# Moving the S5 parameter set-up and two of its four weight sets from the first feed-forward network into the even mixer's output projection

## The chip, the core and the metric

The kernel runs on one core of a Trainium2 chip. Its engines have queues of their own, each worked off in order: TensorE (PE in the profile, its weight loads PEld), VectorE (DVE), ScalarE (ACT), GpSimd (POOL) and SyncE (SP), which only issues DMAs. The metric is the device time of one execution in microseconds (us), median over several runs. All arithmetic is in float32.

## The reference

The reference is a decoder trunk of two layers over a sequence of 512 positions and 1024 channels:

```python
for i in range(DEPTH):                      # DEPTH = 2
    hn = rms_norm(x, mix_norm[i])
    m = even_mixer(hn, ...) if i % 2 == 0 else odd_mixer(hn, ...)
    x = x + m
    x = x + conv_ffn(rms_norm(x, ffn_norm[i]), ...)
return rms_norm(x, final_norm)
```

The even mixer is retention (4 heads) beside a Mamba-2 state-space part (16 heads), joined to 2048 channels (`mix`) and mapped back by the output projection `mix @ w_out`. The odd mixer is a convolution module beside S5, a complex diagonal state-space model with 32 groups of 64 states. S5 needs parameters that depend on the inputs of the kernel alone and not on `x`:

```python
step = exp(log_step); mag = exp(a_re * step)
ab_re, ab_im = mag * cos(a_im * step), mag * sin(a_im * step)
f_re, f_im = ((ab - 1) / a)                 # real and imaginary part
bb = f * b                                  # complex, per state and channel
x[t] = ab * x[t-1] + bb @ u[t]; y = Re(c @ x) + d * u
```

The feed-forward network (FFN) is `(silu(gate) * up) @ w_down` with a convolution of width 3 behind the up-projection.

## The kernel before

The activations are held transposed: eight tiles `x[c]` of 128 channels by 512 positions. Each matrix product is done in three passes, on a split of both operands into a rounded part (`hi`) and the remainder (`lo`): `mm3` (L98) issues hi·hi, hi·lo and lo·hi. A weight block is loaded by SP (L89, tile `wraw`, four buffers), rounded by ACT (L90, `whi`, three buffers), and DVE subtracts (L91, `wlo`, three buffers). PE takes a block of 128 output channels in 12 matmuls where four tiles go in (the even output projection, `outp`, L566), and in 24 where eight go in (the FFN's up-projection).

**The even output projection.** The 16 `mix` tiles are projected four at a time, since groups of them are done at different times. `outs(k0, half)` (L583) takes the four tiles from `k0` on and four of the eight channel blocks; each `outp` ends in a DVE add into `x[c]` (L569, one operand in PSUM). With a third argument, `nst`, the block is the last one for that `x[c]`, and the next norm's work follows: `norm_chunk` (L155) makes `xh` (ACT, L161) and `xl` (DVE, L162) and adds the square (ACT L128 or L131, DVE L132). The last calls are `outs(0, 0)`, `outs(12, 0)`, `outs(4, 0, nst)`, `outs(4, 1)`, `outs(12, 1, nst)`: 20 blocks. The add of the last block of an earlier call, `outs(0, 1)`, is kept as `s5_mark`.

**The FFN's start.** In `ffn` (L172) step i of 22 takes two blocks of the up-projection. Behind the first block comes `norm_end` (L167): eight PE matmuls on the sums of squares (`pstat`, L138), DVE's reciprocal root (L140, L116 to L121), four PE transposes (`prow`, L147), and a DVE copy into `R` (L149). Each block's result is scaled by `R` (DVE L185, one operand in PSUM), convolved (ACT L187, two DVE instructions of L190, both tensor operands in SBUF), and after the pair, the gate (ACT L196, DVE L197) and a split (ACT L95, DVE L96) follow. Between the convolution and the gate, `next(aside)` (L194) runs one step of the generator `s5_prep`.

**The generator** (`s5_prep`, L613). Its first step is the set-up, which is queued behind `s5_mark` on DVE: small operations for `step`, `mag` and the angles (DVE, ACT's sine L670, L671), its tail (DVE L677 to L693), loads into `cdr`, `cdi` and `gt` (POOL DMAs, L696 to L700; DVE negates `cdi`, L698), and on POOL the powers of `ab` and the `bb` (`cmul`, L702 to L708, tile names `s5p`, `s5m`). Later steps call `weights(q)` (L759), a weight set: six POOL operations on 128x512 (L703 to L708 by way of L766) and six DVE products and sums (L768 to L773); `store(q)` (L776): four POOL DMAs to `w2d` (L780), eight PE transposes (L786), two ACT copies, two POOL DMAs to `w1d` (L788), eight small matmuls (pG) and a DVE add (L795); and `rot(h)` (L742). At the end `toep()` (L797) writes `tpd`; its zero stores (L802) need only the tile `zt`. The results go through DRAM and are read in the odd mixer.

**What sets the order.** Program order gives the priority. When the program is built, each engine's queue is ordered by it, and an instruction that isn't ready there gives way to a later one. Most tiles, those of the sets among them, come from one pool with 56 buffers (tag `slot`, L78). With `issue_after(ins)` instructions are queued behind `ins` on its engine.

Of the kernel before, what the change touches and what calls it, by code (L numbers as in the profile page):

```python
# [36 lines left out]
class Trunk:  # L37
# [249 lines left out]
        return st  # L287


    def even(self, st):  # L290
        nc = self.nc
        ins = self.ins
        C = self.c
# [272 lines left out]
        def outp(k0, c, last=None):  # L566
            p = self.pp("po")
            self.proj(p, ins["weo"][c, :, k0 * P:(k0 + 4) * P], mix[k0:k0 + 4])
            add = nc.vector.tensor_tensor(self.x[c], self.x[c], p, op=ALU.add)  # L569
            if last is not None:  # L570
                self.norm_chunk(last, c)
            return add
# [10 lines left out]
        def outs(k0, half, last=None):  # L583
            for c in range(4 * half, 4 * half + 4):
                self.add_mark = outp(k0, c, last)
# [15 lines left out]
        s5_mark = self.add_mark  # L601
        group_norm(1, grp[1], ys[1])
        head(3)
        outs(0, 0)
        outs(12, 0)
        outs(4, 0, nst)
        outs(4, 1)
        outs(12, 1, nst)
        self.add_mark = s5_mark
        return nst  # L610


    def s5_prep(self):  # L613
# [7 lines left out]
        def sm(shape=S16):  # L621
            n_[0] += 1
            return self.s5p.tile(shape, F32, name=f"s5_{n_[0]}")
# [6 lines left out]
        with self.tc.issue_after(self.dma_mark.ins), self.tc.issue_after(self.add_mark.ins):  # L630
# [7 lines left out]
            step, x, th, k, m1, m8, s, c, si, co = [sm() for _ in range(10)]  # L638
# [162 lines left out]
                if i:  # L801
                    dma(self.tpd[n:, :, i, :], zt[n:, :].rearrange("p (b x) -> p b x", b=8))  # L802

        for step in ((), (), (weights, 0), (), (store, 0, weights, 1), (), (store, 1, weights, 2), (), (store, 2, weights, 3),
                     (rot, 0), (store, 3), (rot, 1), ()):
            for f, q in zip(step[::2], step[1::2]):
                f(q)
            yield
# [381 lines left out]
def trunk(tc, ins, out):  # L1190
    from contextlib import ExitStack
    with ExitStack() as ctx:
        k = Trunk(ctx, tc, ins)
        st = k.load_x()
        st = k.even(st)
        st = k.ffn(0, st, "mix1", k.s5_prep())
        st = k.odd(st)
        k.ffn(1, st, "final", out=out)

# [15 lines left out]
```

## Time and profile before

| what | us |
|---|---|
| median of three timed runs (1360.03 to 1362.3) | 1360.99 |
| the profiled execution, its own time | 1361.88 |
| its span | 1360.1 |

By stage, in busy us:

| stretch (us from the span's start) | stage | PE | DVE | ACT | POOL |
|---|---|---|---|---|---|
| 0 to 413.5 | even mixer | 406.35 | 305.21 | 194.74 | 36.94 |
| 413.5 to 674.4 | first FFN, up-projection | 253.78 | 223.12 | 107.55 | 109.47 |
| 674.4 to 793.9 | first FFN, down-projection | 119.50 | 43.63 | 34.25 | 0.00 |
| 793.9 to 986.7 | odd mixer | 190.32 | 126.70 | 78.53 | 0.00 |
| 986.7 to 1360 | second FFN and final norm | 365.51 | 219.90 | 135.66 | 9.14 |

The granted clock of TensorE is 1.00 (full speed) in every stretch. A row of the timeline gives an instruction's start and duration in us, its engine, the line of the kernel, the operation, the tile written and those read, the shape, a count, and in brackets how long its engine had been idle and who ended that. Rows of one kind that follow each other are merged into one with their count.

### The profile page before, as it was taken

To read this page: it belongs to the slowest core of one execution; us is meant where nothing else is said; L and a number is where in the kernel's file an instruction comes from. 1 tells how busy PE (TensorE), PEld (TensorE's weight loads), DVE (VectorE), ACT (ScalarE), POOL (GpSimd) and SP (SyncE) were. 2 spreads that over 40 slices of the span, in tenths; PEclk is the share of its full clock that TensorE was granted. 3 is DMA by queue.
4 is the path that set the end of the run, shared out by engine and by line. 5 is a ranking of instruction groups with operands and counts; after the bars stand their busy time and mean duration, and the time that the engine had idled before them with its cause. 6 is when DMAs were issued, how large, how long until landed. Compare 5 with 4: busy or idle time off the path is not lost.

```text
span 1360.1 us, 17410 instructions
## 1 busy us (share of the span) xinstructions
PE 1335.5 (98%) x6660; PEld 1092.1 (80%) x6660; DVE 918.6 (68%) x1545; ACT 550.7 (40%) x775; POOL 155.6 (11%) x283
## 2 busy tenths in 40 slices
PE   8999999999999989999999999999999999999997
PEld 7778888888888777888888888657888888888887
DVE  5887877679568999977733345586877777774233
ACT  5454545444343444444422323144644444442221
POOL 0210010000306233870000000000000000000000
PEclk9999999999999999999999999999999999999999
DMA  6542223232234333553333335231432333233321
GB/s 224 156 111 84 70 81 123 77 104 83 77 119 142 109 109 109 170 160 97 97 90 96 102 95 197 86 143 55 124 109 93 95 102 98 93 90 96 101 71 62
DMA packets 50532, 146.16 MB, mean 107 GB/s; under 512 B 6544, under 2 KB 7872, under 8 KB 50448
## 3 DMA queue, kind: packets, MB, share of 16 engines
q1 hardware_dynamic: 44288, 127.49, 30.5%
q0 software_dynamic: 5872, 17.37, 4.5%
q8 instruction: 52, 0.85, 0.3%
q14 instruction: 32, 0.26, 0.1%
q10 hardware_dynamic: 288, 0.19, 0.0%
HBM read 135.03 MB, written 9.99 MB: 107 GB/s over the span
## 4 chain that ended last, share of the span: by engine, by line
PE 86%; DVE 10%; issue 2%; ACT 1%; DMA 1%; POOL 0%; DVEq 0%; SPq 0%; ACTq 0%; POOLq 0%
PE pup L102 9%; PE pup L100 9%; PE pup L101 9%; PE pdn L102 6%; PE pdn L100 6%; PE pdn L101 6%; DVE ffa L190 3%; PE po L100 3%; PE pcv L885 3%; PE po L102 3%; PE po L101 3%; DVE wlo L91 2%; PE pxbc L101 1%; PE pxbc L100 1%; PE pxbc L102 1%
## 5 line engine op out<-in xcount | busy, mean ns | idle before, releaser
L90 ACT CAST whi<-wraw 128x1024 fp32r<-128x1024 f32 (+3 forms) x246 | 231.0, 939 | 473.3 <-PE pdn L101 135.3
L91 DVE TENSOR_TENSOR wlo<-wraw,whi 128x1024 fp32r<-128x1024 f32 (+3 forms) x246 | 267.7, 1090 | 141.1 <-ACT whi L90 140.5
L102 PE MATMUL pup<-xh,wlo 128*128 128x512 f32 x704 | 274.6, 390 | 3.6 <-DVE wlo L91 3.6
L100 PE MATMUL pup<-xh,whi 128*128 128x512 f32 x704 | 275.0, 391 | 2.7 <-ACT whi L90 2.7
L101 PE MATMUL pup<-xl,whi 128*128 128x512 f32 x704 | 273.9, 389 | 0.0
L102 PEld LDWEIGHTS pup<-xh,wlo 128*128 128x128 f32 x704 | 132.1, 188 | 33.3 <-DVE wlo L91 5.7
L190 DVE SCALAR_TENSOR_TENSOR ffa<-ffh,c,ffa 128x511 f32<-128x511 f32 (+1 forms) x176 | 155.8, 886 | 2.9
L100 PEld LDWEIGHTS pup<-xh,whi 128*128 128x128 f32 x704 | 132.2, 188 | 30.3 <-ACT whi L90 3.5
L101 PEld LDWEIGHTS pup<-xl,whi 128*128 128x128 f32 x704 | 132.2, 188 | 27.2
L100 PE MATMUL pdn<-acth,whi 128*128 128x512 f32 (+1 forms) x374 | 140.9, 377 | 0.0
L101 PE MATMUL pdn<-actl,whi 128*128 128x512 f32 (+1 forms) x374 | 140.8, 377 | 0.0
L102 PE MATMUL pdn<-acth,wlo 128*128 128x512 f32 (+1 forms) x374 | 140.8, 377 | 0.0
L185 DVE TENSOR_TENSOR ffh<-pup,R 128x512 f32<-128x512 f32 x88 | 60.4, 687 | 57.2 <-PE pup L102 57.0
L232 POOL TENSOR_SCALAR x<-x,c 128x512 f32<-128x512 f32 (+1 forms) x9 | 9.1, 1016 | 738.7 <-ACT acc L128 639.3
L187 ACT ACTIVATE ffa<-ffh,c 128x512 f32<-128x512 f32 x88 | 71.8, 816 | 49.4 <-DVE ffh L185 46.2
L101 PEld LDWEIGHTS pdn<-actl,whi 128*128 128x128 f32 x374 | 70.4, 188 | 13.0
L102 PEld LDWEIGHTS pdn<-acth,wlo 128*128 128x128 f32 x374 | 70.4, 188 | 12.9
L100 PEld LDWEIGHTS pdn<-acth,whi 128*128 128x128 f32 x374 | 70.4, 188 | 12.8
L100 PE MATMUL po<-mh,whi 128*128 128x512 f32 x192 | 75.2, 393 | 0.7 <-ACT mh L95 0.7
L102 PE MATMUL po<-mh,wlo 128*128 128x512 f32 x192 | 75.6, 394 | 0.0
L101 PE MATMUL po<-ml,whi 128*128 128x512 f32 x192 | 75.5, 393 | 0.0
L95 ACT CAST acth<-ffg 128x512 fp32r<-128x512 f32 x44 | 27.3, 620 | 115.4 <-DVE ffg L197 110.8
(416 smaller groups left out, 2224.0 us busy)
## 6 DMA issues: line engine op xcount, KB each, us to landing
wraw<-in_wup_dram SPq DMA_DIRECT2D x88, 512.0 KB, 3.7
wraw<-in_wdn_dram SPq DMA_DIRECT2D x32, 512.0 KB, 3.5
wraw<-in_weo_dram SPq DMA_DIRECT2D x32, 256.0 KB, 3.1
wraw<-in_wxbc_dram SPq DMA_DIRECT2D x12, 512.0 KB, 3.7
wraw<-in_wdn_dram SPq DMA_DIRECT2D x16, 384.0 KB, 3.1
wraw<-in_wz_dram SPq DMA_DIRECT2D x8, 512.0 KB, 3.6
wraw<-in_wg_dram SPq DMA_DIRECT2D x8, 512.0 KB, 3.8
ar<-acd POOLq DMA_DIRECT2D x16, 256.0 KB, 3.9
```

Of the source, the lines that this page charges most:

```text
L90: nc.scalar.copy(hi[:, :n], raw[:, :n])
L91: (eng or nc.vector).tensor_tensor(lo[:, :n], raw[:, :n], hi[:, :n].bitcast(F32), op=ALU.subtract)
L95: self.nc.scalar.copy(hi, src)
L100: mm(out, lhsT=w[0], rhs=x[0], start=start, stop=False)
L101: mm(out, lhsT=w[0], rhs=x[1], start=False, stop=False)
L102: self.mark = mm(out, lhsT=w[1], rhs=x[0], start=False, stop=stop)
L185: nc.vector.tensor_tensor(h, p, st["R"], op=ALU.mult)
L187: nc.scalar.activation(a, h, AF.Identity, scale=dw[:, j, 2:3], bias=db[:, j:j + 1])
L190: nc.vector.scalar_tensor_tensor(a[:, s:], h[:, :T - s], dw[:, j, tap:tap + 1], a[:, s:], op0=ALU.mult, op1=ALU.add)
L232: self.nc.gpsimd.tensor_scalar(self.x[c][:, ts], self.x[c][:, ts], st["g"][:, c:c + 1], 1.0, op0=ALU.mult, op1=ALU.mult)
L885: self.mark = mm(p[64 * g:64 * g + 64, s:], lhsT=w, rhs=cin[i][g][:, :T - s], start=j == 0, stop=j == 15)
```

## The change

The generator is made before the even mixer and handed to it, and its first three steps are taken between the last blocks of the output projection: the set-up behind `outs(0, 0)`, weight set 0 behind `outs(12, 0)`, weight set 1 behind `outs(4, 0, nst)`. `self.add_mark` is set to the same `s5_mark` as before, earlier in the program. The list of steps is changed to go with it: the FFN's step 0 now stores set 0 (before: the set-up), step 1 stores set 1, step 3 makes set 2 (before: step 7), step 5 stores it, step 6 makes set 3 (before: step 9), step 8 stores it; the two rotations come at steps 9 and 11 (before: 10 and 12), and `toep()` at 13 (before: 14).

```diff
-    def even(self, st):
+    def even(self, st, prep):
...
         outs(0, 0)
+        self.add_mark = s5_mark
+        next(prep)
         outs(12, 0)
+        next(prep)
         outs(4, 0, nst)
+        next(prep)
         outs(4, 1)
         outs(12, 1, nst)
-        self.add_mark = s5_mark
         return nst
...
-        for step in ((), (), (weights, 0), (), (store, 0, weights, 1), (), (store, 1, weights, 2), (), (store, 2, weights, 3),
-                     (rot, 0), (store, 3), (rot, 1), ()):
+        for step in ((weights, 0), (weights, 1), (store, 0), (store, 1), (), (weights, 2), (), (store, 2), (weights, 3), (),
+                     (store, 3), (rot, 0), (), (rot, 1), ()):
...
-        st = k.even(st)
-        st = k.ffn(0, st, "mix1", k.s5_prep())
+        prep = k.s5_prep()
+        st = k.even(st, prep)
+        st = k.ffn(0, st, "mix1", prep)
```

## The prediction

> **What bounds the kernel now.** I read the page first, for the engines' shares; then the waits of TensorE (PE) and its order of time around the even mixer's output projection and the first feed-forward network (FFN); then VectorE (DVE) and GpSimd (POOL) in the same stretches, and last the busy time by stretch.
>
> ```profile
> PE 1335.5 (98%) x6660; PEld 1092.1 (80%) x6660; DVE 918.6 (68%) x1545; ACT 550.7 (40%) x775; POOL 155.6 (11%) x283
> ...
> 417.60:560.00 142.40, 135.28 (x631) 110.81 (x630) 131.17 (x165) 53.78 (x72) 69.74 (x103) 1.00 0.42 122
> ```
>
> PE is busy for 98% of the span of 1360.1 us, so the only time to be won without taking work away from PE is its idle time. The second row is the stretch in which the S5 parameters are now computed (columns: busy us of PE, PEld, DVE, ACT, POOL, granted clock, DMA share, GB/s). PE is idle for 142.40 - 135.28 = 7.1 us there; DVE is 92% busy. All of those 7.1 us stand in seven rows:
>
> ```profile
> 424.34 0.65 PE L147 MATMUL prow<-c,rs_y 128*128 128x128 f32 x4 [0.83 <-DVE rs_y L121]
> ...
> 444.51 0.50 PE L102 MATMUL pup<-xh,wlo 128*128 128x512 f32 x1 [0.67 <-DVE wlo L91]
> ...
> 479.07 0.50 PE L102 MATMUL pup<-xh,wlo 128*128 128x512 f32 x1 [1.38 <-DVE wlo L91]
> ...
> 504.99 0.50 PE L100 MATMUL pup<-xh,whi 128*128 128x512 f32 x1 [1.64 <-ACT whi L90]
> ...
> 506.50 0.50 PE L102 MATMUL pup<-xh,wlo 128*128 128x512 f32 x1 [0.78 <-DVE wlo L91]
> ...
> 531.82 0.50 PE L100 MATMUL pup<-xh,whi 128*128 128x512 f32 x1 [1.03 <-ACT whi L90]
> ...
> 533.34 0.50 PE L102 MATMUL pup<-xh,wlo 128*128 128x512 f32 x1 [0.78 <-DVE wlo L91]
> ```
>
> The first is the norm's end (0.83). The others come in four clusters, one behind each weight set: set 0 costs 0.67, set 1 1.38, set 2 1.64 + 0.78 = 2.42, set 3 1.03 + 0.78 = 1.81, together 6.28. In each, PE waits for a weight split that DVE (or ACT, behind DVE) made late. Why DVE was late stands in the rows of POOL and DVE around set 1:
>
> ```profile
> 468.58 0.63 POOL L780 DMA_DIRECT2D w2d<-w2i  x1
> 469.22 1.07 POOL L703 TENSOR_TENSOR w1r<-s5p,s5m 128x512 f32<-128x512 f32 x1
> ...
> 472.28 1.28 POOL L705 TENSOR_TENSOR w1r<-w1r,s5t 128x512 f32<-128x512 f32 x1
> ...
> 475.12 1.62 POOL L708 TENSOR_TENSOR w1i<-w1i,s5t 128x512 f32<-128x512 f32 x1
> ```
>
> ```profile
> 444.98 1.52 DVE L190 SCALAR_TENSOR_TENSOR ffa<-ffh,c,ffa 128x511 f32<-128x511 f32 x2
> ...
> 459.70 0.69 DVE L96 TENSOR_TENSOR actl<-ffg,acth 128x512 fp32r<-128x512 f32 x1 [0.69 <-ACT acth L95]
> ...
> 460.92 0.68 DVE L768 TENSOR_TENSOR w2r<-s5p,s5m 128x512 f32<-128x512 f32 x1
> ...
> 468.72 6.87 DVE L190 SCALAR_TENSOR_TENSOR ffa<-ffh,c,ffa 128x511 f32<-128x511 f32 x2
> 475.69 1.59 DVE L197 TENSOR_TENSOR ffg<-ffg,ffa 128x512 f32<-128x512 f32 x1
> 477.21 0.68 DVE L185 TENSOR_TENSOR ffh<-pup,R 128x512 f32<-128x512 f32 x1
> ```
>
> A weight set is six POOL operations on 128x512, from 469.22 to 475.12 + 1.62 = 476.74. While they run, two L190 and one L197, whose two tensor operands lie in SBUF, take 477.21 - 468.72 = 8.49 us; undisturbed two L190 take 1.52 (444.98), and a product of that size 0.68 (L768). A set therefore takes 8.49 - 2.20 = 6.3 us away from a DVE that has work. An operation of DVE with one operand in PSUM isn't held up:
>
> ```profile
> 565.20 1.06 POOL L703 TENSOR_TENSOR rotc<-rotc,s 128x256 f32<-128x256 f32 x1
> ```
> ```profile
> 565.70 0.68 DVE L185 TENSOR_TENSOR ffh<-pup,R 128x512 f32<-128x512 f32 x1
> ```
>
> **Where the moved work will stand.** The even output projection is 20 blocks of 12 matmuls, and DVE has room in some of them:
>
> ```profile
> 372.90:383.80 10.90, 10.90 (x50) 9.03 (x49) 5.16 (x8) 2.51 (x5) 0.00 (x0) 1.00 0.29 96
> 383.80:394.70 10.90, 10.90 (x49) 9.03 (x49) 9.62 (x15) 7.45 (x13) 0.00 (x0) 1.00 0.30 97
> 394.70:405.50 10.80, 10.80 (x49) 8.93 (x49) 5.25 (x9) 2.45 (x5) 0.00 (x0) 1.00 0.49 147
> 405.50:417.60 12.10, 12.10 (x55) 10.03 (x54) 11.63 (x16) 8.51 (x12) 0.00 (x0) 1.00 0.58 171
> ```
>
> In order these are outs(12,0), outs(4,0) with the norm's pieces, outs(4,1), and outs(12,1) with the norm's pieces. PE never waits; DVE's idle time is 10.90 - 5.16 = 5.74, 1.28, 5.55 and 0.47: half of a plain stretch is free, almost nothing of one with norm pieces.
>
> ```profile
> 372.95 0.69 DVE L569 TENSOR_TENSOR x<-x,po 128x512 f32<-128x512 f32 x1 [1.43 <-PE po L102]
> 373.56 0.69 DVE L91 TENSOR_TENSOR wlo<-wraw,whi 128x512 fp32r<-128x512 f32 x1
> 375.67 0.69 DVE L569 TENSOR_TENSOR x<-x,po 128x512 f32<-128x512 f32 x1 [1.43 <-PE po L102]
> ```
>
> A block is 375.67 - 372.95 = 2.72 us long. The split L91 behind a block's add belongs to the block three later (three wlo buffers); it ends at 374.25, and is first needed by the third matmul of a block that begins about 5.3 us after 372.95: at 378.6. DVE may thus be 4.4 us late before PE stops.
>
> Which of DVE's instructions comes when? The set-up's tail (L677 on) has its inputs from L655 at 341.12, and yet stands directly behind the last norm piece; and set 0's first product (L768, 460.92 above), which belongs to FFN step 3, stands just behind the split of step 2 (L96, 459.70):
>
> ```profile
> 341.12 0.17 DVE L655 SCALAR_TENSOR_TENSOR s<-s,s 128x16 f32<-128x16 f32 x1
> ...
> 368.56 0.68 DVE L96 TENSOR_TENSOR ml<-gs,mh 128x512 fp32r<-128x512 f32 x1
> ...
> 417.02 0.68 DVE L132 TENSOR_TENSOR acc<-acc,sq 128x512 f32<-128x512 f32 x1
> 417.62 0.18 DVE L677 TENSOR_TENSOR s5p<-s,s 128x16 f32<-128x16 f32 x1
> ...
> 419.09 0.18 DVE L692 TENSOR_TENSOR s<-s,s 128x16 f32<-128x16 f32 x1
> ...
> 422.64 0.28 DVE L693 TENSOR_SCALAR s5m<-s5m 128x256 f32<-128x256 f32 x1
> ...
> 428.34 1.18 DVE L698 TENSOR_SCALAR cdi<-cdi 128x512 f32<-128x512 f32 x1 [1.90 <-DMA cdi<-in_s5cdi_dram]
> ```
>
> ```profile
> 417.89 0.22 POOL L703 TENSOR_TENSOR s5p<-s5p 128x16 f32<-128x16 f32 x1 [57.45 <-DVE s5p L678]
> ...
> 430.42 4.24 POOL L802 DMA_DIRECT2D tpd<-s5z  x6
> 434.27 1.47 POOL L703 TENSOR_TENSOR w1r<-s5p,s5m 128x512 f32<-128x512 f32 x1
> ```
>
> I read it so: the tiles of tag "slot" are handed out in program order, and work that needs one follows. With the generator called earlier, L677 comes behind head(3)'s last split (L96, 368.56), near 369 to 371. POOL, which waited 57.45 us for it, needs 434.27 - 417.89 = 16.4 us from there to the first set, of which 4.24 and more are DMA issues that can go ahead; so set 0's POOL stream would begin near 381, and set 1's, which nothing separates from it, near 389, until 397: mostly over outs(4,0), the stretch with 1.28 us of room.
>
> **The sum.** Added to DVE between 371.5 and 417.6: the set-up's tail, 419.09 + 0.18 - 417.62 = 1.65 for L677 to L692, 0.28 for L693 and 1.18 for L698, 3.1 in all (L698's wait of 1.90 for cdi is left out, since the load can be issued earlier; with it 5.0, the upper bound); twelve products L768 to L773 at 0.61, the step from 372.95 to 373.56, 7.3; two POOL streams at 6.3, 12.6. Together 23.0. Against it stand the four idle times, 13.0, and the gap of 1.43 before 372.95: 14.5. At the end the norm's statistics allow a little:
>
> ```profile
> 418.99 0.95 PE L138 MATMUL pstat<-onec,acc 128*128 128x1 f32 x8
> ```
>
> PE comes to them at 418.99, the sum of squares is ready at 417.02 + 0.68 = 417.70: 1.3 more. So 23.0 - 14.5 - 1.3 = 7.2 us of DVE work find no room, and PE waits for it, in front of L91's splits late in outs(4,0) and in outs(4,1), and at pstat. The bounds of a stream's price: below, only the wait of the blocked splits, three per 8 us in plain blocks at 1.28 (L705's length) each, 3.8; above, all 7.5 from 469.22 to 476.74. I take 6.3, measured on this very stream.
>
> Won in the FFN: the norm's 0.83, since the set-up's operations no longer lie among the rsqrt's; I take 0.6, between 0 and 0.83. Of the 6.28, sets 0 and 1 are gone. Sets 2 and 3 now come at steps 3 and 6, their stores at 5 and 8. They may cost nothing, or what sets 2 and 3 cost now, 4.23. The nearest row is set 0, whose POOL stream also lay well ahead of its DVE products: 0.67 each, 1.3. Won: 6.28 - 1.3 = 5.0.
>
> At no cost I put: the two stores moved to steps 0 and 1 (the same transposes and matmuls of PE, copies of ACT and L795, and six POOL DMAs each, whose inputs were ready some 30 us before; if they weren't, PE, in order, would stand at the transposes); SP's queue, which is moved past nothing; and the seven zero stores of toep, POOL DMAs that go earlier and that nobody awaits. POOL's queue holds nothing else in the stretch (busy 0.00 in all four rows), so no DMA of another step is held behind the moved operations. No wait is added in the code; the new one is DVE's for its inputs from POOL, with the splits and adds queued behind it.
>
> Net: 7.2 - 0.6 - 5.0 = +1.6 us. The profiled execution took 1361.88 us (1.78 around its span), 0.9 above the median of the three timed runs, 1360.99. Its own time would become 1363.5; the median 1360.99 + 1.6 = 1362.6. About 0.2%, 2.7 us, is what a measurement of this kernel can tell from no change, so this is a trade that comes out even.
>
> [...]
>
> **The rivals.** *Slower: the FFN gives little back.* The two remaining sets each stand behind a store in POOL's queue, as sets 1 to 3 did, and DVE's six products (3.7 us) come against the stream (6.3), which is what made those sets cost 1.38 to 2.42 where set 0 cost 0.67. Price: the FFN still loses 4.23, and wins 2.05 instead of 5.0: 7.2 - 0.6 - 2.05 = +4.55, 1365.5. It decides from where the two cost over 2.4 us together (1.3, and the 1.1 from +1.6 to +2.7). For it: POOL's queue is in order, and a store's L780 waits for DVE. Against: a step without a set lies between. If the room of outs(4,1) also comes too late for the streams (5.55 less set 1's products, 3.7, so 1.9 more), 1367.4.
>
> *Faster: POOL can't hold DVE so long here.* Ahead of the stream at 469.22 POOL was issuing a DMA (L780, 468.58), in which L190 was already caught; in the projection no DMA need precede it, and if DVE gets in between POOL's instructions, a stream costs only 3.8: 23.0 - 12.6 + 7.6 - 15.8 = 2.2, and 2.2 - 0.6 - 5.0 = -3.4, 1357.6. Against it: L190 didn't get in between L703 and L705, where no DMA stood. [...]
>
> *Nothing moves:* the slots of the sets come free only at the end of the projection, POOL's streams stay at the FFN's start, and the time stays 1361. For it: this work waited for slots before (L677 above). Against: eight mix tiles are free after outs(0,0).
>
> **How the numbers follow.** Forecast 0.36, its own range 1360 to 1365 (the FFN's 0 to 4.23 around 1.3 cut at half); nothing moves 0.04; slower 0.36, since it needs only sets 2 and 3 to cost what they cost now; faster 0.24. So faster 0.24, same 0.40, slower 0.36. The range goes from a little below the faster case, 1356.5 (it, with sets 2 and 3 free, -1.3), to 1368, the slower case with the room missed.
>
> **What would show it.** Right: L677 near 369; POOL busy from 370 to 400; PE rows with 3 to 7 us of idle time in all, behind L91 between 385 and 410 and at pstat; L147's wait below 0.4; two clusters instead of four in the FFN, under 1 us each. Wrong: no idle PE in the projection (the streams' price falls), or clusters of 1.5 us and more behind sets 2 and 3, or POOL's streams still behind 417.

## The result and the profile after

The changed kernel takes 1368.72 us (median of four runs, 1368.68 to 1368.93) beside 1360.60 of the kernel before on the same chip: a ratio of 1.0060, 95% interval 1.0048 to 1.0073, so 8.1 us slower, outside the range given. (Lines from L609 on stand three further down in the changed kernel: L677 is L680, L698 is L701, L703 is L706, L768 is L771.)

First the engines' shares, then what TensorE waited for between 365 and 580 us (columns: us in total, times, longest), then the stretch of the FFN in which it was idle for 7.1 us before:

```profile
PE 1338.7 (98%) x6660; PEld 1095.0 (80%) x6660; DVE 913.2 (67%) x1545; ACT 551.3 (40%) x775; POOL 158.8 (12%) x283
```
```profile
PE po L102 <- DVE wlo L91: 11.3, 3, 5.7
```
```profile
417.60:560.00 142.40, 142.40 (x682) 119.27 (x682) 113.12 (x153) 62.59 (x83) 44.21 (x63) 1.00 0.46 134
```

The FFN's idle time is gone altogether (142.40 of 142.40), more than I gave it. Against that stand three stops, all in the projection, 11.3 us. In order of time, with what DVE and POOL did ahead of them:

```profile
384.67 0.80 PE L102 MATMUL po<-mh,wlo 128*128 128x512 f32 x1 [5.65 <-DVE wlo L91]
...
403.86 0.50 PE L102 MATMUL po<-mh,wlo 128*128 128x512 f32 x1 [2.53 <-DVE wlo L91]
...
414.31 0.66 PE L102 MATMUL po<-mh,wlo 128*128 128x512 f32 x1 [3.12 <-DVE wlo L91]
```
```profile
367.27 0.18 DVE L680 TENSOR_TENSOR s5p<-s,s 128x16 f32<-128x16 f32 x1
...
373.17 0.69 DVE L569 TENSOR_TENSOR x<-x,po 128x512 f32<-128x512 f32 x1 [1.31 <-PE po L102]
377.98 2.55 DVE L701 TENSOR_SCALAR cdi<-cdi 128x512 f32<-128x512 f32 x1 [4.12 <-DMA cdi<-in_s5cdi_dram]
380.45 4.17 DVE L91 TENSOR_TENSOR wlo<-wraw,whi 128x512 fp32r<-128x512 f32 x1
...
395.56 1.62 DVE L162 SCALAR_TENSOR_TENSOR xl<-x,c,xh 128x512 fp32r<-128x512 f32 x1 [0.19 <-ACT xh L161]
397.11 5.23 DVE L132 TENSOR_TENSOR acc<-acc,sq 128x512 f32<-128x512 f32 x1
...
408.76 0.69 DVE L771 TENSOR_TENSOR w2r<-s5p,s5m 128x512 f32<-128x512 f32 x1
...
413.57 0.69 DVE L91 TENSOR_TENSOR wlo<-wraw,whi 128x512 fp32r<-128x512 f32 x1
```
```profile
374.53 0.54 POOL L700 DMA_DIRECT2D cdi<-in_s5cdi_dram  x1
...
378.52 1.05 POOL L706 TENSOR_TENSOR w1r<-s5p,s5m 128x512 f32<-128x512 f32 x1
...
390.80 1.31 POOL L783 DMA_DIRECT2D w2d<-w2r  x2 [3.26 <-DVE w2r L773]
...
397.20 1.33 POOL L706 TENSOR_TENSOR w1r<-s5p,s5m 128x512 f32<-128x512 f32 x1
```

The first: DVE, which works its queue off in order, waits 4.12 us for `cdi`, whose load POOL issues only at 374.53, behind its powers of `ab`; then set 0's stream (from 378.52) holds L701 (2.55) and the split L91 (4.17). The second: set 1's stream (from 397.20) holds L132 (5.23). The third: set 1's six products and two adds stand in front of L91.

The stops aren't all. The next view is the busy time in stretches of 3.413 us; why this grid, is told below. The first pair is PE's busy us and matmuls, the clock is third from the end:

```profile
380.36:383.78 3.42, 0.00 (x0) 0.00 (x0) 3.42 (x2) 0.00 (x0) 3.41 (x4) 1.00 0.08 10
383.78:387.19 3.41, 2.52 (x6) 2.03 (x7) 3.41 (x4) 0.00 (x0) 3.40 (x5) 0.50 0.42 95
387.19:390.60 3.41, 3.41 (x9) 2.64 (x9) 3.41 (x6) 0.62 (x1) 0.35 (x1) 0.50 0.37 107
390.60:394.02 3.42, 3.42 (x16) 2.81 (x16) 3.42 (x6) 1.68 (x3) 2.12 (x4) 1.00 0.44 141
...
400.84:404.26 3.42, 0.89 (x5) 0.43 (x4) 3.42 (x4) 1.28 (x3) 3.26 (x3) 1.00 0.00 1
404.26:407.67 3.41, 3.41 (x10) 2.65 (x9) 3.22 (x5) 1.40 (x3) 0.69 (x1) 0.50 0.24 77
407.67:411.08 3.41, 3.41 (x16) 2.57 (x14) 3.41 (x6) 1.87 (x4) 0.00 (x0) 1.00 0.23 77
411.08:414.50 3.42, 0.30 (x2) 0.19 (x2) 3.42 (x7) 0.09 (x1) 1.88 (x3) 1.00 0.40 77
414.50:417.91 3.41, 3.41 (x9) 2.66 (x9) 1.55 (x3) 0.00 (x0) 0.70 (x2) 0.50 0.68 156
```

Behind each stop PE is granted half the clock for one or two such stretches, and a full one then holds 9 or 10 matmuls instead of 16. PE is "busy" there, so no view of waits shows it. Lost: half of 2.52 + 3 x 3.41, 6.4 us.

Together 11.3 + 6.4 - 7.1 = +10.6. The profiled execution of before had come to the projection some 2.3 us later than that of the changed kernel, with nothing changed ahead of it (the first matmul of `pxbc` by L102 starts at 21.72 there and at 19.42 in the changed kernel; L147 starts at 424.34, and in run e3 below, which changes nothing ahead of it either, at 421.99), which leaves 8.3.

```profile
421.99 0.65 PE L147 MATMUL prow<-c,rs_y 128*128 128x128 f32 x4 [0.83 <-DVE rs_y L121]
```

Those 2.3 us come from the clock at the start of the run. PE begins at 5.06 us in the execution of before and at 4.92 in that of the changed kernel, but its matmuls come twice as close (0.13 us from start to start instead of 0.23) only from 12.86 us on in the one and from 8.31 in the other; half of the difference is 2.3 us. At these times the clock record of the two traces has its first entry, so the 1.00 that a view gives for the time ahead of it says nothing; the counts of matmuls in the same stretch do (before, then after):

```profile
9.00:11.00 2.00, 2.00 (x9) 2.00 (x10) 2.00 (x4) 2.00 (x5) 0.00 (x0) 1.00 1.05 393
```
```profile
9.00:11.00 2.00, 2.00 (x19) 2.00 (x18) 2.00 (x4) 2.00 (x4) 0.00 (x0) 1.00 1.05 390
```

The spans differ by 6.8, 1.5 us less than the 8.3. Half of that lies in how a row counts idle time, from the modelled end of the matmul before it: from start to start the stops cost 11.8 us here and 8.3 before. The rest stays open.

### The profile page after: what moved, and what is told of

The parts are those of the page before. It is cut to its first block, busy times and chain, and to the rows that moved or that the text cites. A ratio compares the mean times of both kernels' runs of the same rounds, so it can differ in the third digit from the quotient of the medians.

```text
span 1366.9 us, 17413 instructions
## 1 busy us (share of the span) xinstructions
PE 1338.7 (98%) x6660; PEld 1095.0 (80%) x6660; DVE 913.2 (67%) x1545; ACT 551.3 (40%) x775; POOL 158.8 (12%) x283
## 4 chain that ended last, share of the span: by engine, by line
PE 92%; DVE 5%; ACT 1%; issue 1%; DMA 0%; POOL 0%; DVEq 0%; ACTq 0%; POOLq 0%
PE pup L100 12%; PE pup L102 12%; PE pup L101 12%; PE pdn L100 6%; PE pdn L102 6%; PE pdn L101 6%; PE pcv L888 3%; PE po L100 2%; PE po L102 2%; PE po L101 2%; PE pxbc L101 1%; PE pxbc L100 1%; PE pxbc L102 1%; PE pyd L454 1%; PE pqk L100 1%; PE pqk L102 1%
## 5 line engine op out<-in xcount | busy, mean ns | idle before, releaser
L91 DVE TENSOR_TENSOR wlo<-wraw,whi 128x1024 fp32r<-128x1024 f32 (+3 forms) x246 | 271.9, 1107 | 141.3 <-ACT whi L90 140.9
L102 PE MATMUL pup<-xh,wlo 128*128 128x512 f32 x704 | 274.0, 389 | 0.0
L102 PEld LDWEIGHTS pup<-xh,wlo 128*128 128x128 f32 x704 | 132.1, 188 | 27.5
L102 PE MATMUL pdn<-acth,wlo 128*128 128x512 f32 (+1 forms) x374 | 140.8, 377 | 0.0
L190 DVE SCALAR_TENSOR_TENSOR ffa<-ffh,c,ffa 128x511 f32<-128x511 f32 (+1 forms) x176 | 135.9, 773 | 3.0
L102 PE MATMUL po<-mh,wlo 128*128 128x512 f32 x192 | 78.3, 408 | 11.3 <-DVE wlo L91 11.3
L102 PEld LDWEIGHTS pdn<-acth,wlo 128*128 128x128 f32 x374 | 70.4, 188 | 12.9
```

Source lines behind the costliest of these rows:

```text
L91: (eng or nc.vector).tensor_tensor(lo[:, :n], raw[:, :n], hi[:, :n].bitcast(F32), op=ALU.subtract)
L102: self.mark = mm(out, lhsT=w[1], rhs=x[0], start=False, stop=stop)
L190: nc.vector.scalar_tensor_tensor(a[:, s:], h[:, :T - s], dw[:, j, tap:tap + 1], a[:, s:], op0=ALU.mult, op1=ALU.add)
```

## Experiments

Line numbers are those of each run's own kernel (L703 of before is L704 in e2 and L706 in e12). *Lookahead* is how late DVE may be before PE stops, 4.4 us by the prediction.

Theory A: DVE's lateness makes the stops, in pieces (the wait for `cdi` with set 0's stream, set 1's stream, its products), and TensorE's clock is halved behind each long one. Rival B: the amount of DVE work and the streams count, wherever the pieces are cut. Rival C: the lower clock costs nothing.

**The disputed cost by itself.** 18 idle DVE additions (nobody reads them) in the kernel before, in one piece, then in two.

```diff
         outs(0, 0)
+        hold(18)                # e6: hold(9)
         outs(12, 0)
         outs(4, 0, nst)
+                                # e6: hold(9)
```

> The kernel before with nothing moved and 18 extra DVE additions of 128x512 in one piece behind outs(0,0), on tiles that nobody reads: 18 x 0.61 = 11.0 us in which the splits wait. Less the gap of 1.43 us and the lookahead of 4.4 us that makes one TensorE stop of about 5.2 us. Theory A (the clock is granted by fixed windows of 3.41 us, and is halved behind a window in which TensorE worked less than about 0.45 of the time, for one to three windows): a stop of 5 us always empties one window, so that the time grows by 5.2 + 1.7 to 3.4 for each half-clock window or two, 7 to 9 us in all: 1367 to 1369. Rival C (a granted clock of 0.50 is a matter of record): 5.2 us, 1365.4.

Measured: 1366.86, ratio 1.0047 (1.0034 to 1.0059), +6.5 us. The timeline of DVE and the stretches of the grid (PE first, clock third from the end):

```profile
369.73 10.92 DVE L609 TENSOR_TENSOR dyb<-dya 128x512 f32<-128x512 f32 x18
```
```profile
377.47:380.89 3.42, 0.00 (x0) 0.00 (x0) 3.42 (x7) 0.00 (x0) 0.00 (x0) 1.00 0.00 0
380.89:384.30 3.41, 2.92 (x7) 2.17 (x8) 3.35 (x6) 0.00 (x0) 0.00 (x0) 0.50 0.06 19
384.30:387.71 3.41, 3.41 (x17) 2.83 (x16) 1.29 (x2) 0.62 (x1) 0.00 (x0) 1.00 0.63 210
```

The stop was 4.8 us, near the 5.2 of gap and lookahead, and half clock followed for one window, 1.5 us. Theory A's 3.41 us is the grid of the changed kernel's trace, and its 0.45 lies between a window busy for 0.42 in e4 that half clock followed and one busy for 0.46 in e3 that full clock followed. By the total alone the rival's 5.2 isn't excluded; the count of matmuls, and e4 below, exclude it.

> The same 18 additions as two pieces of 9, behind outs(0,0) and behind outs(4,0): 5.5 us each. Theory A: each is under the gap of 1.43 us and the lookahead of 4.4 us together, so TensorE stops for under 0.5 us in all, no window is emptied, and the time stays within 1 us of the kernel before, 1360 to 1361: the room of the projection is real, if it is used in pieces. Rival B (the amount of work counts, 11 us against a room that the norm's pieces use up): half of the cost of the one piece, 1363 and more.

Measured: 1362.52, ratio 1.0014 (1.0006 to 1.0023), +2.1: between the two. PE stopped 0.15 us behind the first piece, and 1.11 + 0.41 behind the second, which follows the norm's pieces, where DVE arrives late. The same work costs a third in two pieces. The interval, 1361.2 to 1363.5, still holds the rival's 1363; that the cut matters at all is shown by 2.1 beside 6.5.

**One cause of the first stop taken away.** The loads of `cdr`, `cdi`, `gt` go out behind the set-up's first loads.

```diff
                 nc.gpsimd.dma_start(t_, ins[n])
...
+            dma(cdr, ins["s5cdr"])
+            dma(cdi, ins["s5cdi"])
...
+            dma(gt, ins["s5dd"])
...
-            dma(cdr, ins["s5cdr"])
-            dma(cdi, ins["s5cdi"])
...
-            dma(gt, ins["s5dd"])
```

> Only the issue of the three small loads (cdr, cdi, gt) moves: behind the set-up's first loads instead of behind POOL's power chain. Theory A (in-order wait plus clock): DVE's 4.12 us wait for cdi goes, the first stop of TensorE in the projection falls from 5.65 us to under 2, and the half clock of some 6 us behind it (2.9 us lost) goes with it: about 7 us less than the changed kernel, 1361 to 1363; the stops of 2.53 and 3.12 us stay, each with half clock behind. Rival B (only the amount of DVE work and the POOL streams count): the wait is filled, but the stream of set 0 then meets the same splits, so at most the 4 us come back and more likely 1 to 2: 1365 to 1368. Rival C (the granted clock is a matter of record and costs nothing): 4 us, 1364.5, with the matmuls' spacing as in the changed kernel.

Measured: 1366.76, ratio 1.0049 (1.0037 to 1.0062): only 2.0 less than the changed kernel (1.5, each taken beside its own runs of the kernel before), the rival's number. The wait is gone, and with DVE earlier at them, the products of set 0 met the stream in front of the adds:

```profile
380.79 2.99 DVE L771 TENSOR_TENSOR w2r<-s5p,s5m 128x512 f32<-128x512 f32 x1
383.70 4.04 DVE L772 TENSOR_TENSOR s5u<-s5p,s5m 128x512 f32<-128x512 f32 x1
387.67 1.82 DVE L774 TENSOR_TENSOR w2i<-s5p,s5m 128x512 f32<-128x512 f32 x1
```

One piece of 9 us; stops of 3.1 and 3.8 follow, and one of 4.9 behind splits that set 1's stream held (6.28 us for two): 11.8 us in sum, no less than the 11.3 with the wait. That the wait for `cdi` by itself cost the first stop, as I held, falls.

**Less of the change.** e2 moves the set-up alone, and calls the sets at the FFN's steps of the kernel before; e4 leaves set 1 to the FFN's step 0.

```diff
         outs(12, 0)
-        next(prep)              # e2 only
         outs(4, 0, nst)
-        next(prep)
```

> Only the set-up is moved into the projection; the sets stay at the FFN's steps of the kernel before. Theory A: the 4.12 us wait for cdi stands in front of the splits, but no stream follows it, so that of the 4.4 us that DVE may be late little is exceeded: one stop of 0 to 2 us, no half clock behind it; the norm's 0.83 us in the FFN goes, the four clusters (6.3 us) stay: 1360 to 1362, no difference to the kernel before. Rival B (the set-up by itself is what makes the first stop): a stop of 4 us and more and half clock: 1366 and more.

Measured: 1356.38, ratio 0.9971 (0.9961 to 0.9982), 3.8 faster and below theory A's 1360 to 1362, which had left all four of the FFN's clusters standing. The wait for `cdi` (3.86) makes a stop of 1.43 us, at full clock (1.00 from 378 to 392); in the FFN one cluster was left of four (1.0 + 0.8). Set 0, called at FFN step 3, ran in the projection all the same, since POOL's queue held nothing else:

```profile
384.71 1.46 POOL L704 TENSOR_TENSOR w1r<-s5p,s5m 128x512 f32<-128x512 f32 x1
```
```profile
384.73 5.26 DVE L91 TENSOR_TENSOR wlo<-wraw,whi 128x512 fp32r<-128x512 f32 x1
```

It held a split for 5.26 us, and PE stopped for 0.15 us: one hold alone is all but covered.

> Set-up and set 0 stay in the projection, set 1 goes back to the FFN's step 0. Theory A: the first stop (5.65 us and half clock behind it) stays, the second and third (2.53 and 3.12 us, and 3.4 us of half clock) go: 9 us less than the changed kernel, 1359 to 1361, a little faster than before or equal, if the FFN's three sets cost nothing. Rival C (half clock costs nothing): 5.7 us less, 1363.

Measured: 1363.44, ratio 1.0022 (1.0013 to 1.0031): 5.3 less than the changed kernel (4.8, each taken beside its own runs of the kernel before), the rival's number, but not for its reason. Two stops stayed, 9.0 us in sum, the longer one 5.6, since set 1's stream, called later, began at 398.23 all the same (397.20 in the changed kernel), over L132; only the products' stop went. This run shows the cost of the clock. Its eleven executions differ in their mean granted clock, and in time with it:

| mean granted clock | executions | us |
|---|---|---|
| 0.997 | 2 | 1360.96, 1361.08 |
| 0.995, 0.996 | 6 | 1362.94 to 1363.70 |
| 0.994 | 3 | 1364.56 to 1364.75 |

0.003 of 1363 us are 4.1 us; the time grows by 3.6. With the counts of matmuls above, the granted clock is no mere record. The mean alone would not show it: in the kernel before, executions at 0.997 and at 0.998 take the same time (1359 to 1361 us), and five of eight at 0.999 take longer, 1361.7 to 1362.6; the mean leaves out the time ahead of the clock record's first entry.

**The FFN's side.** e3 moves nothing, and spaces the steps.

```diff
-        for step in ((), (), (weights, 0), (), (store, 0, weights, 1), (), (store, 1, weights, 2), ...
+        for step in ((weights, 0), (), (store, 0), (weights, 1), (), (store, 1), (weights, 2), ...
```

> Nothing is moved into the projection; in the FFN the four sets and the four stores stand in steps of their own (sets at steps 1, 4, 7, 10, stores at 3, 6, 9, 12). Theory A (what the FFN won came from the spacing, not from having two sets fewer): all four clusters go, PE idle time in the FFN falls from 7.1 us to about 1: 1354 to 1356. Rival B (it came from having two sets fewer there): the sets that DVE's products follow at once still cost 0.7 to 2.4 each, 1358 to 1361.

Measured: 1358.15, ratio 0.9985 (0.9976 to 0.9994), the rival's end: stops of 0.83, 0.59, 0.46 and 2.87 were left. The last shows that length alone doesn't decide on the clock:

```profile
476.07:479.48 3.41, 2.39 (x11) 1.66 (x9) 3.41 (x7) 1.76 (x2) 1.32 (x2) 1.00 0.24 43
479.48:482.89 3.41, 1.56 (x7) 1.29 (x8) 3.41 (x5) 0.92 (x2) 1.25 (x2) 1.00 0.65 95
482.89:486.31 3.42, 3.42 (x17) 2.81 (x16) 2.59 (x5) 1.44 (x3) 0.00 (x0) 1.00 0.82 303
```

It falls over two windows, of which neither is emptied (busy for 0.70 and 0.46), and the clock stays at 1.00; behind the 2.53 us in the changed kernel, all in one window (busy for 0.26), it was 0.50.

**No POOL stream at all.** The sets' six multiplications and sums go to DVE: e7 in the changed kernel; e8 with set-up alone moved and loaded early, sets at FFN steps 0, 3, 6, 9; e11 the same sets with nothing moved.

```diff
...
-            cmul(v(w1r), v(w1i), pw(qr), pw(qi), mt(bbr), mt(bbi), v(t1))
+            cmul(v(w1r), v(w1i), pw(qr), pw(qi), mt(bbr), mt(bbi), v(t1), nc.vector.tensor_tensor)
```

> The changed kernel with the six multiplications and sums of every weight set on DVE instead of POOL; places and steps as in the changed kernel. DVE then has 12 x 0.61 = 7.3 us a set and no stream holds it, instead of 3.7 of its own and 5.2 to 6.3 held. Theory A (the streams' holds, in one piece each, make the stops; the half clock follows from their length): stops of 1 to 3 us behind the wait for cdi and behind the second set, 2 to 6 us in all, at most one or two half-clock windows: 1354 to 1361, 1357 likeliest. Rival B (the place is full, whoever does the work): the three stops stay as they are, 1366 to 1369.

Measured: 1366.02, ratio 1.0041 (1.0027 to 1.0054), the rival's side: five stops, 7.9 us, and a mean granted clock of 0.994, as in the changed kernel's trace. Eleven of set 1's twelve instructions came as one piece, from 403.69 to the add at 410.32, and the next rows of DVE show three adds and three splits caught up one behind the other:

```profile
409.72 0.68 DVE L775 TENSOR_TENSOR s5u<-s5p,s5m 128x512 f32<-128x512 f32 x1
410.32 0.68 DVE L569 TENSOR_TENSOR x<-x,po 128x512 f32<-128x512 f32 x1
410.92 0.68 DVE L776 TENSOR_TENSOR w2i<-w2i,s5u 128x512 f32<-128x512 f32 x1
411.52 1.28 DVE L569 TENSOR_TENSOR x<-x,po 128x512 f32<-128x512 f32 x2
412.71 1.89 DVE L91 TENSOR_TENSOR wlo<-wraw,whi 128x512 fp32r<-128x512 f32 x3
```

So the streams are not the root either: a piece of 7 us of DVE's own work at this place stops PE as well.

> Set-up alone in the projection, with its three small loads issued early; all four sets in the FFN, on DVE, at steps 0, 3, 6 and 9, and each store in a step of its own. Theory A: no stop in the projection, and 0 to 2 us of idle time of TensorE in the FFN in place of 7.1: 1352 to 1355. Rival B (12 instructions of DVE in one piece are 7.3 us, more than the splits may be late): a stop of 1 to 2.5 us for each set, 1356 to 1361.

Measured: 1350.95, ratio 0.9928 (0.9916 to 0.9941), 9.5 us faster than before: the version that beats both. PE waits for nothing between 365 and 580 us. The same twelve instructions a set that stop PE in the projection cost nothing in the up-projection; a likely reason is that a `wlo` buffer there holds a block of 24 matmuls (twice 2.72 us), here one of 12.

> Nothing moved into the projection; the four sets in the FFN on DVE, at the same distance from each other as in the run with the early set-up (1350.95). It tells what the move of the set-up is worth by itself. Theory A: the norm's 0.83 us stays and the sets cost nothing: 1351.5 to 1353. Rival: the set-up in the FFN makes DVE and POOL late for set 0, a stop of 1 to 3 us: 1353 to 1356.

Measured: 1355.80, ratio 0.9961 (0.9947 to 0.9975), the rival's number: a stop of 2.1 us behind set 0 and the norm's 0.8 (mean granted clock 0.997 in this trace, 0.998 in e8's). Moving the set-up, with its loads issued early, is worth the 4.9 us to e8.

**More lookahead.** Four buffers instead of three for `whi` and `wlo`, in the changed kernel (e9) and in the kernel before (e10).

```diff
-        hi = self.wp.tile([P, 1024], F32R, name="whi", tag="whi", bufs=3)
-        lo = self.wp.tile([P, 1024], F32R, name="wlo", tag="wlo", bufs=3)
+        hi = self.wp.tile([P, 1024], F32R, name="whi", tag="whi", bufs=4)
+        lo = self.wp.tile([P, 1024], F32R, name="wlo", tag="wlo", bufs=4)
```

> The changed kernel with four buffers instead of three for the split weights (whi and wlo), so that a split may run one block further ahead: 2.72 us more in the projection, 7.1 instead of 4.4. Theory A (a stop is what a piece of DVE work exceeds the lookahead by, and half clock follows where a window is emptied): the stops of 5.65, 2.53 and 3.12 us fall by up to 2.7 each, to about 2.9, 0 and 0.4, and two or three of the five half-clock windows go: 7 to 12 us less than the changed kernel, 1357 to 1362. Rival B (DVE has too much work in the projection; buffers don't help): the lateness adds up, stops of 9 to 11 us stay, 1365 to 1369.

Measured: 1368.14, ratio 1.0053 (1.0040 to 1.0065), no gain, and the rival's number. The first stop fell from 5.65 to 2.93, one block as expected; at the second place another limit took over:

```profile
PE po L102 <- DVE wlo L91: 4.5, 2, 2.9
PE po L100 <- DVE x L569: 4.0, 2, 3.3
```

PE then waits for the adds of `po` that stand behind the held L132 (5.21 us; there are four such accumulators), and the mean granted clock stays at 0.994.

> The kernel before with the same four buffers, as the control of the run beside it: the four clusters behind the sets in the FFN (6.3 us) are a lateness of DVE as well; a block there is 5.45 us, and one more buffer covers more than the longest of them (2.42). Theory A: the 6.3 us go, the norm's 0.83 stays: 1353 to 1355. Rival B: no difference, 1360.

Measured: 1354.66, ratio 0.9958 (0.9946 to 0.9971), as theory A had it: one stop of 1.7 and the norm's 0.9 were left. In the FFN lookahead alone wins back 4.5 of the 7.1 us of idle time that the change won there.

**A set in pieces.** As e8, but set 0's products go behind the second block of outs(12, 0), the rest of it behind the first of outs(4, 1).

```diff
+                if c == at:
+                    next(prep)
...
-        outs(12, 0)
+        outs(12, 0, at=1)
         outs(4, 0, nst)
-        outs(4, 1)
+        outs(4, 1, at=4)
```

> Set-up (loads early) and set 0 in the projection, set 0 on DVE in two pieces of six instructions, 3.7 us each: the products behind the second block of outs(12, 0), the other six behind the first block of outs(4, 1), where DVE is idle half of the time; sets 1 to 3 in the FFN on DVE. Theory A (a piece under the gap of 1.43 and the lookahead of 4.4 costs nothing): no stop in the projection, the time of the run with set-up alone moved, 1350 to 1352. Rival B (the projection has no room for a set, whoever does it and in whatever pieces): a stop of 1 to 4 us there, 1352 to 1358.

Measured: 1355.37, ratio 0.9960 (0.9948 to 0.9973): one stop of 2.1 us, and 4.4 us more than e8, whose trace has no stop there. That is the rival's number, but neither theory's reason: the first product waited, in order, 2.96 us for POOL's powers, and three of the other five took 1.16 to 1.28 us instead of 0.68.

```profile
375.80 0.69 DVE L770 TENSOR_TENSOR w2r<-s5p,s5m 128x512 f32<-128x512 f32 x1 [2.96 <-POOL s5p L708]
```

The second piece cost nothing.

## Why the prediction was wrong

- **Where the work goes: right, but for set 1's stream.** L680 came at 367.27 (369 to 371 predicted), set 0's stream at 378.52 (381). Set 1's came at 397.20 instead of 389: I wrote that nothing separates them, but the store's DMAs stood between in POOL's queue and waited 3.26 us for DVE's products. That put set 1's stream over the norm's pieces at the end of outs(4, 0), where L132 was held. Why the queue has the store first, no run shows.
- **The price of the streams: right.** DVE's rows between 367 and 420 are 12.3 us longer in sum than undisturbed ones of their kind, without L701 (2.55 beside 0.41 in e12); predicted 12.6. The rival "POOL can't hold DVE so long" falls (4.17, 5.23).
- **The room: the first step that failed.** I set 23.0 us of work against 15.8 of room as one sum, and left out the wait for `cdi`, "since the load can be issued earlier". It is issued by POOL behind its powers, and cost 4.12 us of that room; the stops were 11.3 instead of 7.2. That 7.2 and 4.1 add up to 11.3 is chance: e1 has no such wait, and stops of 11.8. The sum itself fails in e5, where 11.0 us of work, well inside 15.8 of room, stopped PE for 4.8. What decides is how far each piece (a wait, a hold, own work, or two of them that meet) goes beyond what the splits run ahead: one hold is all but free (e2), 11 us cost 4.8 of stop in one piece and 1.7 in two (e5, e6), 7 us of plain DVE work stop PE as a stream does (e7).
- **The clock: missing from the sum.** 6.4 us, most of the miss. No stop before exceeded 1.64 us, and that trace has half clock only at its two ends: until 12.86 us, where the clock record is silent and only the matmuls' spacing shows it, and from 1357.71 on (0.50), behind PE's last matmul (1352.25 to 1353.18). The sum priced every stop at its length alone.
- **The FFN: too small.** 5.6 predicted, 7.1 measured; sets 2 and 3 cost nothing, not 0.67 each. The rival of the slower side ("the FFN gives little back") had the right sign for a reason that fell. Of the 7.1 us in the profiled executions, spacing by itself gives 2.4 (e3), lookahead 4.5 (e10), the absence of the set-up and of set 0, which came early with it, 5.3 (e2).
- **Put at no cost:** the two stores and the zero stores. PE waits for none of them, but the store's DMAs put off set 1's stream, as said. The one wait that I named as new, DVE's for its inputs from POOL, I gave no price; it came to 4.12 us, for a load that POOL issues.

In numbers: +7.2 - 5.6 = +1.6 predicted; +11.3 + 6.4 - 7.1 = +10.6 in the traces, 8.1 timed.

## What to carry to other kernels

Idle time of an in-order engine is no budget to be summed (11.0 us of work in 15.8 of room stopped PE for 4.8 in e5): ask for each piece of moved work, with the waits in front of it, whether it is shorter than the lookahead of what stands behind it at that very place. Ask what its inputs wait for, and note that a step on an empty queue (POOL here) starts when its inputs are there, not where the program calls it (set 0 in e2, at 384.71). Don't price a stop of TensorE at its length alone: by the counts of matmuls, half clock added 6.4 us to 11.3 of stops in the changed kernel, and 1.5 to one of 4.8 in e5.

## What the runs showed of the hardware

In the changed kernel's trace the granted clock changes at 383.78, 390.60, 404.26, 407.67, 414.50 and 417.91 us, and behind PE's last work at 1363.40: 2, 4, 1, 2, 1 and 277 times 3.413 us apart, and the record's first entry, 8.31, lies 110 times that ahead of the first of them. In the trace of before the only two entries, 12.86 and 1357.71, are 394 times 3.413 us apart.

Laid on that grid, windows at full clock that were followed by half clock had PE busy for 0.00, 0.26 and 0.09 of the time in the changed kernel, 0.13 and 0.42 in e4, 0.00 and 0.35 in e5. Windows followed by full clock were busy for 0.61 in the changed kernel, 0.70 and 0.59 in the kernel before, 0.70 and 0.46 in e3, 0.75 in e5. So a window need not be empty; where the limit lies, so few don't show. The cluster behind set 2 in the FFN (1.6 + 0.8 us of stops) passed at full clock in the kernel before, where it fell over two windows (0.70 and 0.59 busy), and was followed by half clock in e5, where PE was busy for 0.35 of one. The full clock came back behind a window busy for 0.86 (e5), and not behind one of 0.74 (the changed kernel) or of 0.60 (e4).

The grid does not lie at the same place in each execution: PE starts at 5.06 us in the trace of before and at 4.92 in that of the changed kernel, and the first full clock comes at 12.86 and at 8.31. How a stop lies on the grid counts beside its length: 2.87 us in e3, over two windows, left the clock at 1.00, and 2.53 in the changed kernel, in one, did not. This may also be why e4's executions differ by 3.8 us; only one of them was traced.
